# Transposes taken one by one from a list of those due, between the 512-column products, in a one-core encoder block

## The chip, the core and the metric

The kernel runs on one core of a Trainium2 chip. Time is device time in microseconds (us). The kernel before takes 1980.33 us, the median of 3 runs (1980.31 to 1980.41).

## What is computed

One encoder layer on 256 tokens of 2048 channels, float32:

```python
x = x + 0.5 * swiglu(rmsnorm(x), w_gate1, w_up1, w_down1)      # hidden layer 5632
h = rmsnorm(x)
u, v, g = split(h @ w_in)                                      # 1024, 2048, 4096 columns
a = pool_branch(u)          # centred window means by 4 groups, w_group, scale, w_proj
b = conv_branch(v)          # GLU, depthwise conv 31, LayerNorm, silu, w_proj
x = x + (sigmoid(g_a) * a + sigmoid(g_b) * b) @ w_out
x = x + 0.5 * swiglu(rmsnorm(x), w_gate2, w_up2, w_down2)
out = rmsnorm(x)
```

Nearly all of the work is matrix products of 256 tokens with the weights, 378 MB that pass through once.

## The kernel before

**Tiling.** The weights come as one stream of chunks. A chunk is two row tiles of 128 x 1024. A `Unit` is a run of chunks that adds up to x[256, K] @ w[K, 1024]: 8 chunks for K = 2048, 22 for the down projections, 4 for the two projections of the branches (K = 1024). Each row tile is split on the way into a high part wh (a cast on ScalarE, L135) and a low part wl (a subtraction on VectorE, L137), and so is each left operand. A product is one matmul of 512 columns at L208. Each row tile takes 12 of them, in `products` (L203): two token tiles t, three pairs of high and low parts, two column halves c. So a chunk has 24 products.

**Accumulators.** The two token tiles of a unit have an accumulator each (two PSUM banks), and three such buffers take turns. The second token tile of a unit is given the buffer that held the first token tile of the unit before. In the last chunk of a unit the 12 products of token tile 0 come first, then those of token tile 1.

**Order.** `run` writes for every chunk: the loads of a later chunk on SP's queue, the split of the next chunk (two casts on ScalarE, two subtractions on VectorE), then the small work that was put down for this chunk with `at`, then the chunk's products; small work put down with `amid` stands between the 12th and the 13th product. Each engine takes its instructions in the order in which they are written.

**Transposes.** The products need their left operand with channels on partitions. `transposes` (L245) takes one of two PSUM banks (pool `ps_t`), and writes four 128 x 128 transposes into it one after the other (L250): two column blocks of two token tiles. Its callers read the bank at once:

- hT: the feed-forward's hidden layer (`gate_done`, L288). Each of the 22 units of the two gate/up stages gives two groups of four, before the products of the second and of the third chunk of the next unit. One cast and one subtraction of 128 x 512 read the bank.
- xt: the residual (`x_transposed`, L254), after each half of the first feed-forward's residual and of the mixer's. Two banks in a row, so eight transposes, before the products of a chunk. Each bank is read by two pairs of a ScalarE operation (L241) and a VectorE operation (L242).
- gT: the gated convolution input (L383), eight in the middle of a chunk, read by one ScalarE copy for each bank (L385).
- mT: the gated sum of the two branches (`cp_done`, L615), eight in the middle of a chunk, read by two pairs of cast and subtraction (mAh, mAl or mBh, mBl) for each bank. The mT of the first half stand in the third and in the fourth, which is the last, chunk of the second w_cp unit. After that chunk `cp_done` adds a row to the accumulators of this unit on VectorE (L606, conv<-acc), token tile 0 first, and so gives the buffers back. The next unit is the first of w_out.

Of the kernel before, what the change touches and what calls it, by code (L numbers as in the profile page):

```python
# [13 lines left out]
P = 128  # L14
D = 2048
T = 256
NT = T // P
# [17 lines left out]
WARM = 9  # L35
# after these row tiles of weights, the row tiles of x^T that are loaded
XT_LOADS = {(0, 0): (1, 2), (0, 1): (2, 4), (1, 0): (4, 8), (2, 0): (8, 12), (3, 0): (12, 16)}
TAPS = 6
TAPS_BUSY = 4

# columns of the packed per-partition vectors
V_N1, V_NM, V_N2 = 0, KD, 2 * KD
# [8 lines left out]
class Unit:  # L51
    """x[T, K*128] @ w[K*128, 1024]: K row tiles, two banks of 512 columns for each token tile."""

# [5 lines left out]
class Special:  # L59
    """A chunk of the weight stream with a use of its own."""  # L60

# [5 lines left out]
def encoder_kernel(ctx: ExitStack, tc: tile.TileContext, x, xT, vecs, rows, pool_m,  # L67
                   w_g1, w_d1, w_in, w_pg, w_pp, w_cp, w_out, w_g2, w_d2, out):
    nc = tc.nc
# [9 lines left out]

    # ---------------------------------------------------------------- constants and small state  # L80
    ident = const.tile([P, P], F32, name="ident")
# [10 lines left out]

    # ---------------------------------------------------------------- the stream of weight chunks
    stream = []
    side, middle = {}, {}

    def at(i, fn):
        """fn is emitted before the products of chunk i."""
        side.setdefault(i, []).append(fn)

    def amid(i, fn):
        """fn is emitted between the products of chunk i."""
        while isinstance(stream[i][0], Special):
            i += 1
        middle.setdefault(i, []).append(fn)
# [60 lines left out]
    def bank(name):  # L166
        return ps_t.tile([P, C], F32, tag="T", name=name)

    def run_chunk(i):
        u, cc = stream[i]  # L170
        if isinstance(u, Special):
            u.use(split.pop(i))
            return
        if cc == 0:
            n = NT + 1 if u.tail else NT
            u.acc = [ps_a.tile([P, 2, C], F32, tag="acc", name=f"acc{i}_{t}") for t in range(n)]
        ws = split.pop(i)
        left = u.k // 2 - 1 - cc
        if u.tail and left < 2:
            # the last two chunks: token tile 0, then token tile 1 by columns  # L180
            for kk in range(2):
                products(u, 2 * cc + kk, 0, ws[kk])
            if left:
                u.kept = ws
                return
            u.tail(0, (0, 1), u.acc[0])
            for c in range(2):
                for kk in range(4):
                    products(u, 2 * cc - 2 + kk, 1, (u.kept + ws)[kk], (c,))
                u.tail(1, (c,), u.acc[1 + c])  # L190
            return
        order = [(kk, t) for kk in range(2) for t in range(NT)]
        if not left:
            order.sort(key=lambda o: o[1])
        for n, (kk, t) in enumerate(order):
            if n == 2:
                for fn in middle.pop(i, []):
                    fn()
            products(u, 2 * cc + kk, t, ws[kk])
        if not left:  # L200
            u.done(u.acc)

    def products(u, k, t, w, cs=(0, 1)):  # L203
        xh, xl = u.lhs(k, t)
        wh, wl = w
        for n, (a, b) in enumerate(((xh, wh), (xh, wl), (xl, wh))):
            for c in cs:
                nc.tensor.matmul(  # L208
                    u.acc[t + c if u.tail and t else t][:, c, :],
                    lhsT=a,  # L210
                    rhs=b[:, c * C:(c + 1) * C],
                    start=k == 0 and n == 0,
                    stop=k == u.k - 1 and n == 2,
                )

    # ---------------------------------------------------------------- operands of the products
    def pair(pool, tag, n, name):
        """hi and lo by row tile, four row tiles to a block."""
        r = []
        for b in range(n // 4):  # L220
            h, l = (block(pool, f"{tag}{s}{b}", F32R, f"{name}{s}{b}") for s in "hl")
            r += [(h[:, q, :], l[:, q, :]) for q in range(4)]
        return r
# [4 lines left out]
    def hidden(pool, name):  # L228
        """The feed-forward's hidden layer, hi and lo by row tile, four of them in a block."""
        return [tuple(block(pool, f"h{s}{u}", F32R, f"{name}{s}{u}") for s in "hl") for u in range(FF // C)]  # L230
# [7 lines left out]
    def scaled_split(dst, src, gain):  # L238
        """dst = hi and lo of src * gain, a scalar of each partition."""
        h, l = dst  # L240
# [3 lines left out]

    def transposes(src_of, n, name):  # L245
        """n (up to 4 / NT) tiles [T, 128] into one bank as [128, T] each."""
        b = bank(name)
        for j in range(n):
            for t in range(NT):
                nc.tensor.transpose(out=b[:, j * T + t * P: j * T + (t + 1) * P],  # L250
                                    in_=src_of(j, t), identity=ident)
        return b

    def x_transposed(dst, gain_base, k0):  # L254
        """dst[k0], dst[k0 + 1] = the transposed residual times the gain."""
        b = transposes(lambda j, t: X[t][:, (k0 + j) * P:(k0 + j + 1) * P], 2, f"xt{Pos.now}_{k0}")
        for j in range(2):
            scaled_split(dst[k0 + j], b[:, j * T:(j + 1) * T], vcol(gain_base, k0 + j))

# [11 lines left out]

    # ---------------------------------------------------------------- feed-forward
    def ffn_units(w_g, w_d, xt, ht, rs, residual_done, tail=None):
# [3 lines left out]
        def gate_done(u):  # L277
            def done(acc):
# [9 lines left out]
                def put(k0):  # L288
                    b = transposes(lambda j, t: hs[t][:, (k0 + j) * P:(k0 + j + 1) * P], 2,
                                   f"hT{Pos.now}_{k0}")  # L290
                    hi_lo(b.rearrange("p (q t) -> p q t", q=2), *(h[:, k0:k0 + 2, :] for h in ht[u]))
                at(Pos.now + 2, lambda: put(0))
# [19 lines left out]
    def next_operand(xt, gain_base, rs):  # L312
        """After each half of the residual: its transposed tiles, and in the end the row norms."""
        def f(half):
# [6 lines left out]

    # ---------------------------------------------------------------- pass 0: what starts the stream
    xt1 = pair(xtp, "x", KD, "xt1")
# [20 lines left out]

    # ---------------------------------------------------------------- plan
    def run(first, last):
# [9 lines left out]

    # phase 1
    ht_stack = ExitStack()
# [5 lines left out]

    # phase 2 units are appended before phase 1 runs, so that the weights run ahead
    mix = {}
# [5 lines left out]
    def v_done(j):  # L372
        def done(acc):
# [9 lines left out]
            def put(k0):  # L383
                b = transposes(lambda q, t: gl[t][:, (k0 + q) * P:(k0 + q + 1) * P], 2, f"gT{j}_{k0}")
                nc.scalar.copy(out=mix["gluT"][:, 4 * j + k0:4 * j + k0 + 2, :],  # L385
                               in_=b.rearrange("p (q t) -> p q t", q=2))
            amid(Pos.now + 1, lambda: put(0))
# [41 lines left out]
    def ln_mean():  # L429
        """LayerNorm over the channels (partitions and tiles), spread over the chunks from here."""  # L430
        cv, cp = mix["conv"], conv_pairs()
# [93 lines left out]
    def use_pool_m(ws):  # L525
        """pooled^T = u^T M^T, M the window's sum less count times the token itself."""
        def group(g):
# [69 lines left out]
    def cp_done(half):  # L597
        def done(acc):
# [16 lines left out]
            def put(k0):  # L615
                b = transposes(lambda q, t: gates[half, t][:, (k0 + q) * P:(k0 + q + 1) * P], 2,
                               f"mT{half}_{k0}")
                for q in range(2):
                    hi_lo(b[:, q * T:(q + 1) * T], *mix["m"][8 * half + k0 + q])
            for q in range(4):  # L620
# [33 lines left out]

    # phase 3 units
    ht2 = []
    fin = {}

    def final_tail(t, cs, acc):
        """The last of the residual, its norm and what is stored, for columns cs of token tile t."""  # L660
        pieces = [(c, 0, C) for c in cs] if t == 0 else [(c, a, T) for c in cs for a in (0, T)]
# [35 lines left out]

    # ---------------------------------------------------------------- run
    xr = [block(htp, f"h{s}{FF // C - 1 - j}", F32, f"xr{s}{j}") for j in range(2) for s in "hl"]
# [44 lines left out]
def _pack(w, cols):  # L744
    """[K*128, N] -> [units, K, 128, 1024]: cols[u] lists the column ranges of unit u."""
    import numpy as np
# [9 lines left out]
def _pool_constants():  # L756
    """M^T by window (tokens on partitions), and one over the counts."""
    import numpy as np
# [68 lines left out]
```

## Time and profile before

| | |
|---|---|
| median of 3 runs | 1980.33 us |
| span of the profiled execution, first to last instruction | 1978.6 us |
| what the median has beyond that span | 1.7 us |
| TensorE busy | 1966.4 us, 99% |
| VectorE busy | 1110.4 us, 56% |
| ScalarE busy | 874.5 us, 44% |
| transposes | 288: 176 hT, 64 xt, 32 mT, 16 gT |

The profile is of one execution. Of this execution the page gives the span alone, so its own time is read as the span and the 1.7 us around it. A busy TensorE says only that something was in its pipe; how long one instruction holds the engine is read from the distance between the starts of its instructions in the timeline. The timeline merges instructions of one kind that follow one another, with their count (x2, x8).

### The profile page before, as it was taken

To read this page: it belongs to the slowest core of one execution; us is meant where nothing else is said; L and a number is where in the kernel's file an instruction comes from. 1 tells how busy PE (TensorE), PEld (TensorE's weight loads), DVE (VectorE), ACT (ScalarE), POOL (GpSimd) and SP (SyncE) were. 2 spreads that over 40 slices of the span, in tenths; PEclk is the share of its full clock that TensorE was granted. 3 is DMA by queue.
4 is the path that set the end of the run, shared out by engine and by line. 5 is a ranking of instruction groups with operands and counts; after the bars stand their busy time and mean duration, and the time that the engine had idled before them with its cause. 6 is when DMAs were issued, how large, how long until landed. Compare 5 with 4: busy or idle time off the path is not lost.

```text
span 1978.6 us, 22916 instructions
## 1 busy us (share of the span) xinstructions
PE 1966.4 (99%) x8848; PEld 1629.5 (82%) x8848; DVE 1110.4 (56%) x1224; ACT 874.5 (44%) x997; POOL 11.0 (1%) x22
## 2 busy tenths in 40 slices
PE   9999999999999999999999999999999999999998
PEld 7888888888888888888888888888888888888886
DVE  5454544444445445888897765555544444444444
ACT  6444444444434345454444544544444444443433
POOL 0000000000000000000000000000000000000000
PEclk9999999999999999999999999999999999999999
DMA  8555555555555656666666555555555555565564
GB/s 310 193 188 196 190 192 188 187 189 190 192 191 187 195 189 202 194 195 211 202 208 205 184 185 185 181 186 198 191 188 189 189 190 192 181 198 195 192 192 149
DMA packets 106141, 383.88 MB, mean 194 GB/s; under 512 B 11920, under 2 KB 12176, under 8 KB 105776
## 3 DMA queue, kind: packets, MB, share of 16 engines
q1 hardware_dynamic: 104688, 378.45, 58.4%
q0 software_dynamic: 1056, 3.83, 0.6%
q8 instruction: 69, 1.13, 0.2%
q14 instruction: 40, 0.33, 0.1%
q10 hardware_dynamic: 288, 0.14, 0.0%
HBM read 380.28 MB, written 2.10 MB: 193 GB/s over the span
## 4 chain that ended last, share of the span: by engine, by line
PE 99%; DMA 1%; issue 0%; ACT 0%; DVE 0%; DVEq 0%; POOLq 0%; POOL 0%; ACTq 0%
PE acc L208 96%; PE hT L250 1%; PE xt L250 0%; DMA raw<-in_w_g 0%; PE mixb L560 0%; DMA xrh<-in_xT 0%; PE pool L535 0%; PE mT L250 0%; PE gT L250 0%; ACT fsq L668 0%; ACT wh L135 0%; PE ln_mean L442 0%; PE ln_var L471 0%; DVE X L680 0%; DVE X L665 0%
## 5 line engine op out<-in xcount | busy, mean ns | idle before, releaser
L137 DVE TENSOR_TENSOR wl<-raw,wh 128x1024 fp32r<-128x1024 f32 (+1 forms) x706 | 853.8, 1221 | 741.7 <-ACT wh L135 741.5
L135 ACT CAST wh<-raw 128x1024 fp32r<-128x1024 f32 (+1 forms) x706 | 736.2, 1050 | 906.9 <-PE acc L208 849.6
L208 PE MATMUL acc<-wh,xt1h 128*128 128x512 f32 x704 | 219.2, 392 | 1.8 <-ACT wh L135 0.9
L208 PE MATMUL acc<-wh,xt3h 128*128 128x512 f32 x704 | 218.9, 392 | 0.0
L208 PE MATMUL acc<-wl,xt1h 128*128 128x512 f32 x704 | 217.4, 390 | 0.1
L208 PE MATMUL acc<-wl,xt3h 128*128 128x512 f32 x704 | 217.1, 390 | 0.0
L208 PE MATMUL acc<-wh,xt1l 128*128 128x512 f32 x704 | 216.9, 389 | 0.0
L208 PE MATMUL acc<-wh,xt3l 128*128 128x512 f32 x704 | 216.8, 389 | 0.0
L208 PEld LDWEIGHTS acc<-wl,xt1h 128*128 128x128 f32 x704 | 132.1, 188 | 28.1 <-DVE wl L137 0.4
L208 PEld LDWEIGHTS acc<-wh,xt1l 128*128 128x128 f32 x704 | 132.1, 188 | 28.2 <-DVE xt1l L242 0.5
L208 PEld LDWEIGHTS acc<-wh,xt3l 128*128 128x128 f32 x704 | 132.1, 188 | 27.8
L208 PEld LDWEIGHTS acc<-wl,xt3h 128*128 128x128 f32 x704 | 132.1, 188 | 27.8
L208 PEld LDWEIGHTS acc<-wh,xt1h 128*128 128x128 f32 x704 | 130.6, 188 | 28.6 <-ACT wh L135 1.5
L208 PEld LDWEIGHTS acc<-wh,xt3h 128*128 128x128 f32 x704 | 130.5, 188 | 25.8
L208 PE MATMUL acc<-wh,xt2h 128*128 128x512 f32 x448 | 138.3, 390 | 0.0
L208 PE MATMUL acc<-wl,xt2h 128*128 128x512 f32 x448 | 138.1, 389 | 0.0
L208 PE MATMUL acc<-wh,xt2l 128*128 128x512 f32 x448 | 138.0, 389 | 0.0
L208 PE MATMUL acc<-wh,ht2h 128*128 128x512 f32 x352 | 109.2, 390 | 0.0
L208 PE MATMUL acc<-wl,ht2h 128*128 128x512 f32 x352 | 109.1, 389 | 0.0
L208 PE MATMUL acc<-wh,ht2l 128*128 128x512 f32 x352 | 109.0, 389 | 0.0
L208 PE MATMUL acc<-wh,ht1h 128*128 128x512 f32 x352 | 108.7, 390 | 0.0
L208 PE MATMUL acc<-wh,ht1l 128*128 128x512 f32 x352 | 108.4, 389 | 0.0
(144 smaller groups left out, 1699.9 us busy)
## 6 DMA issues: line engine op xcount, KB each, us to landing
raw<-in_w_g SPq DMA_DIRECT2D x350, 512.0 KB, 3.3
raw<-in_w_d SPq DMA_DIRECT2D x176, 512.0 KB, 3.5
raw<-in_w_in SPq DMA_DIRECT2D x112, 512.0 KB, 4.2
raw<-in_w_out SPq DMA_DIRECT2D x32, 512.0 KB, 4.2
raw<-in_w_pp SPq DMA_DIRECT2D x16, 512.0 KB, 4.0
raw<-in_w_cp SPq DMA_DIRECT2D x16, 512.0 KB, 4.0
row<-in_rows POOLq DMA_DIRECT2D x7, 512.0 KB, 4.2
X<-in_x SPq DMA_DIRECT2D x2, 1024.0 KB, 8.9
```

The lines of the kernel that those rows point to most:

```text
L135: nc.scalar.copy(out=h, in_=src)
L137: nc.vector.tensor_tensor(out=l, in0=src, in1=h.bitcast(F32), op=ALU.subtract)
L208: nc.tensor.matmul(u.acc[t + c if u.tail and t else t][:, c, :], lhsT=a, rhs=b[:, c * C:(c + 1) * C], start=k == 0 and n == 0, stop=k == u ...
L250: nc.tensor.transpose(out=b[:, j * T + t * P: j * T + (t + 1) * P], in_=src_of(j, t), identity=ident)
```

## The change

`transposes` no longer issues anything. It puts its transposes into a list `between`, and whoever reads the bank is now a function that is called behind the last transpose of the bank. `products` takes one transpose off the list after each 512-column product:

```diff
+    between = []
...
     def products(u, k, t, w, cs=(0, 1)):
...
             for c in cs:
                 nc.tensor.matmul(
...
                 )
+                if between:
+                    between.pop(0)()
...
-    def transposes(src_of, n, name):
-        b = bank(name)
-        for j in range(n):
-            for t in range(NT):
-                nc.tensor.transpose(out=b[:, j * T + t * P: j * T + (t + 1) * P],
-                                    in_=src_of(j, t), identity=ident)
-        return b
+    def transposes(src_of, n, name, use):
+        got = []
+
+        def one(j, t):
+            if not got:
+                got.append(bank(name))
+            nc.tensor.transpose(out=got[0][:, j * T + t * P: j * T + (t + 1) * P],
+                                in_=src_of(j, t), identity=ident)
+            if (j, t) == (n - 1, NT - 1):
+                use(got[0])
+        between.extend(lambda j=j, t=t: one(j, t) for j in range(n) for t in range(NT))
```

The callers for hT, xt, gT and mT hand what they did with the bank over as `use`, for hT:

```diff
-                    b = transposes(lambda j, t: hs[t][:, (k0 + j) * P:(k0 + j + 1) * P], 2,
-                                   f"hT{Pos.now}_{k0}")
-                    hi_lo(b.rearrange("p (q t) -> p q t", q=2), *(h[:, k0:k0 + 2, :] for h in ht[u]))
+                    transposes(lambda j, t: hs[t][:, (k0 + j) * P:(k0 + j + 1) * P], 2, f"hT{Pos.now}_{k0}",
+                               lambda b: hi_lo(b.rearrange("p (q t) -> p q t", q=2),
+                                               *(h[:, k0:k0 + 2, :] for h in ht[u])))
```

On TensorE the first group of hT, ahead of chunk 9, stands like this before (hT9 is the bank, h7 the hidden layer of two token tiles, acc8 the accumulators, wh9 and wl9 the weights, xt1h and xt1l the left operand; x2 are the two column halves):

```order
L250 MATMUL hT9_0_584<-ident_78,h7_0_504 128x128
L250 MATMUL hT9_0_584<-ident_78,h7_1_508 128x128
L250 MATMUL hT9_0_584<-ident_78,h7_0_504 128x128
L250 MATMUL hT9_0_584<-ident_78,h7_1_508 128x128
L208 MATMUL acc8_0_546<-wh9_0_515,xt1h0_90 128x512 x2
L208 MATMUL acc8_0_546<-wl9_0_516,xt1h0_90 128x512 x2
L208 MATMUL acc8_0_546<-wh9_0_515,xt1l0_91 128x512 x2
```

and like this after:

```order
L209 MATMUL acc8_0_546<-wh9_0_515,xt1h0_90 128x512
L256 MATMUL hT9_0_585<-ident_78,h7_0_504 128x128
L209 MATMUL acc8_0_546<-wh9_0_515,xt1h0_90 128x512
L256 MATMUL hT9_0_585<-ident_78,h7_1_508 128x128
L209 MATMUL acc8_0_546<-wl9_0_516,xt1h0_90 128x512
L256 MATMUL hT9_0_585<-ident_78,h7_0_504 128x128
L209 MATMUL acc8_0_546<-wl9_0_516,xt1h0_90 128x512
L256 MATMUL hT9_0_585<-ident_78,h7_1_508 128x128
L209 MATMUL acc8_0_546<-wh9_0_515,xt1l0_91 128x512 x2
```

The four transposes moved behind the first, second, third and fourth product of the chunk; each now has a product on both sides.

The second place is the second mT group, in the middle of chunk 205, the last of the second w_cp unit. On TensorE before (mT0_4 and mT0_6 are the two banks, gate0 the gated sum, acc202_1 the accumulator of token tile 1, yh and yl the left operand; in brackets, the engines whose semaphores an instruction waits for):

```order
L250 MATMUL mT0_4_8558<-ident_78,gate0_0_6769 128x128 [waits DVE_49,PE_49]
L250 MATMUL mT0_4_8558<-ident_78,gate0_1_6772 128x128
L250 MATMUL mT0_4_8558<-ident_78,gate0_0_6769 128x128
L250 MATMUL mT0_4_8558<-ident_78,gate0_1_6772 128x128
L250 MATMUL mT0_6_8567<-ident_78,gate0_0_6769 128x128 [waits DVE_49,PE_49]
L250 MATMUL mT0_6_8567<-ident_78,gate0_1_6772 128x128
L250 MATMUL mT0_6_8567<-ident_78,gate0_0_6769 128x128
L250 MATMUL mT0_6_8567<-ident_78,gate0_1_6772 128x128
L208 MATMUL acc202_1_8417<-wh205_0_8484,yh1_7163 128x512 x2
```

and after, from the fifth product of token tile 1 on:

```order
L209 MATMUL acc202_1_8417<-wh205_0_8484,yl1_7164 128x512
L256 MATMUL mT0_6_8572<-ident_78,gate0_0_6769 128x128 [waits DVE_49,PE_49]
L209 MATMUL acc202_1_8417<-wh205_0_8484,yl1_7164 128x512
L256 MATMUL mT0_6_8572<-ident_78,gate0_1_6772 128x128
L209 MATMUL acc202_1_8417<-wh205_1_8488,yh1_7163 128x512
L256 MATMUL mT0_6_8572<-ident_78,gate0_0_6769 128x128
L209 MATMUL acc202_1_8417<-wh205_1_8488,yh1_7163 128x512
L256 MATMUL mT0_6_8572<-ident_78,gate0_1_6772 128x128
L209 MATMUL acc202_1_8417<-wl205_1_8489,yh1_7163 128x512 x2
```

The last transpose of the second bank moved from ahead of all twelve products to behind the eighth. The order of the instructions on ScalarE, VectorE, GpSimd and SP is the same before and after, at all places; only TensorE's changes. The first product of the w_out unit into its second token tile (six products into the unit) waits for VectorE, before and after.

## Rows read from the trace of the kernel before

**Rows 1.** The page's first line, its busy times by engine, and the shares of the chain that ended last.

```profile
span 1978.6 us, 22916 instructions
...
PE 1966.4 (99%) x8848; PEld 1629.5 (82%) x8848; DVE 1110.4 (56%) x1224; ACT 874.5 (44%) x997; POOL 11.0 (1%) x22
...
PE 99%; DMA 1%; issue 0%; ACT 0%; DVE 0%; DVEq 0%; POOLq 0%; POOL 0%; ACTq 0%
```

**Rows 2.** The view of waits for TensorE, complete: who waited for whom, us in total, times, longest.

```profile
PE warm L707 <- DVE ones L326: 1.1, 1, 1.1
PE acc L208 <- ACT wh L135: 0.9, 1, 0.9
PE acc L208 <- ACT xt1h L241: 0.9, 1, 0.9
```

**Rows 3.** The transposes by the tile that they write: count, shortest, median and longest ns from start to end of one, first and last start in us.

```profile
L250 PE MATMUL hT<-ident,h x176: 270/272/273, 57.4 to 1740.6; 128*128 128x128 f32 x176
...
L250 PE MATMUL xt<-ident,X x64: 270/272/273, 622.8 to 1251.3; 128*128 128x128 f32 x64
...
L250 PE MATMUL gT<-ident,glu x16: 270/273/273, 787.0 to 832.1; 128*128 128x128 f32 x16
...
L250 PE MATMUL mT<-ident,gate x32: 270/272/273, 1138.1 to 1168.8; 128*128 128x128 f32 x32
```

**Rows 4.** The timeline of TensorE's matmuls around a group of four hT: start, us from the first start to the last end, operation, count. Two products stand in a row, so the distance between two rows' starts is two products.

```profile
56.51 0.62 PE L208 MATMUL acc<-wl,xt1h 128*128 128x512 f32 x2
56.97 0.62 PE L208 MATMUL acc<-wh,xt1l 128*128 128x512 f32 x2
57.43 0.60 PE L250 MATMUL hT<-ident,h 128*128 128x128 f32 x4
57.78 0.71 PE L208 MATMUL acc<-wh,xt1h 128*128 128x512 f32 x2
58.33 0.63 PE L208 MATMUL acc<-wl,xt1h 128*128 128x512 f32 x2
58.80 0.62 PE L208 MATMUL acc<-wh,xt1l 128*128 128x512 f32 x2
```

**Rows 5.** The same around a group of eight xt.

```profile
622.33 0.62 PE L208 MATMUL acc<-wh,ht1l 128*128 128x512 f32 x2
622.79 1.03 PE L250 MATMUL xt<-ident,X 128*128 128x128 f32 x8
...
624.12 0.63 PE L208 MATMUL acc<-wl,ht1h 128*128 128x512 f32 x2
```

**Rows 6.** The timeline of ScalarE and VectorE behind the group of four hT of rows 4; in brackets the engine's idle time ahead of the instruction and what ended it.

```profile
58.58 0.58 ACT L135 CAST ht1h<-hT 128x512 fp32r<-128x512 f32 x1
...
59.85 0.68 DVE L137 TENSOR_TENSOR ht1l<-hT,ht1h 128x512 fp32r<-128x512 f32 x1
...
60.83 1.05 ACT L135 CAST wh<-raw 128x1024 fp32r<-128x1024 f32 x1 [1.67 <-PE acc L208]
```

**Rows 7.** The timeline of ScalarE and VectorE around the group of eight xt of rows 5.

```profile
620.65 4.65 DVE L137 TENSOR_TENSOR wl<-raw,wh 128x1024 fp32r<-128x1024 f32 x4 [1.81 <-ACT wh L135]
...
625.22 0.48 DVE L242 SCALAR_TENSOR_TENSOR xt2l<-xt,vec,xt2h 128x256 fp32r<-128x256 f32 x1
...
625.73 0.84 ACT L241 ACTIVATE xt2h<-xt,vec 128x256 fp32r<-128x256 f32 x2 [1.32 <-DVE xt2l L242]
```

**Rows 8.** The timeline of TensorE, ScalarE and VectorE from the second mT group, in the last chunk of the second w_cp unit (ends at 1148.06), into the first w_out unit.

```profile
1144.45 1.03 PE L250 MATMUL mT<-ident,gate 128*128 128x128 f32 x8
...
1145.09 0.37 ACT L135 CAST mAh<-mT 128x256 fp32r<-128x256 f32 x1 [2.01 <-PE mT L250]
...
1145.49 0.43 DVE L137 TENSOR_TENSOR mAl<-mT,mAh 128x256 fp32r<-128x256 f32 x1 [0.97 <-ACT mAh L135]
...
1145.79 0.62 PE L208 MATMUL acc<-wl,yh 128*128 128x512 f32 x2
1145.95 0.65 ACT L135 CAST mAh<-mT 128x256 fp32r<-128x256 f32 x2 [0.49 <-DVE mAl L137]
...
1147.14 0.37 ACT L135 CAST mAh<-mT 128x256 fp32r<-128x256 f32 x1 [0.54 <-DVE mAl L137]
...
1147.55 0.42 DVE L137 TENSOR_TENSOR mAl<-mT,mAh 128x256 fp32r<-128x256 f32 x1 [0.44 <-ACT mAh L135]
...
1147.89 2.34 DVE L606 TENSOR_TENSOR conv<-acc,row 128x1024 f32<-128x1024 f32 x2
1148.06 0.62 PE L208 MATMUL acc<-wh,mAh 128*128 128x512 f32 x2
...
1149.42 0.62 PE L208 MATMUL acc<-wh,mAh 128*128 128x512 f32 x2
...
1150.15 2.35 DVE L137 TENSOR_TENSOR wl<-raw,wh 128x1024 fp32r<-128x1024 f32 x2
```

**Rows 9.** The timeline of TensorE and ScalarE at the first gT group.

```profile
786.95 1.03 PE L250 MATMUL gT<-ident,glu 128*128 128x128 f32 x8
...
787.59 1.07 ACT L385 COPY gluT<-gT 128x512 f32<-128x512 f32 x2 [0.58 <-PE gT L250]
...
788.55 1.06 ACT L135 CAST wh<-raw 128x1024 fp32r<-128x1024 f32 x1
```

More of the change, by code (lines that the diff above doesn't have):

```diff
@@ L243, in scaled_split, with use @@
                                        op0=ALU.mult, op1=ALU.subtract)
-    def transposes(src_of, n, name):
-        b = bank(name)
-        for j in range(n):
-            for t in range(NT):
-                nc.tensor.transpose(out=b[:, j * T + t * P: j * T + (t + 1) * P],
-                                    in_=src_of(j, t), identity=ident)
-        return b
+    def transposes(src_of, n, name, use):
[8 more added lines that the diff above has]
+        between.extend(lambda j=j, t=t: one(j, t) for j in range(n) for t in range(NT))
     def x_transposed(dst, gain_base, k0):
-        b = transposes(lambda j, t: X[t][:, (k0 + j) * P:(k0 + j + 1) * P], 2, f"xt{Pos.now}_{k0}")
-        for j in range(2):
-            scaled_split(dst[k0 + j], b[:, j * T:(j + 1) * T], vcol(gain_base, k0 + j))
+        def use(b):
+            for j in range(2):
+                scaled_split(dst[k0 + j], b[:, j * T:(j + 1) * T], vcol(gain_base, k0 + j))
+        transposes(lambda j, t: X[t][:, (k0 + j) * P:(k0 + j + 1) * P], 2, f"xt{Pos.now}_{k0}", use)
     def squares(t, slot, c0, c1):
@@ L383, in put @@
             def put(k0):
-                b = transposes(lambda q, t: gl[t][:, (k0 + q) * P:(k0 + q + 1) * P], 2, f"gT{j}_{k0}")
-                nc.scalar.copy(out=mix["gluT"][:, 4 * j + k0:4 * j + k0 + 2, :],
-                               in_=b.rearrange("p (q t) -> p q t", q=2))
+                transposes(lambda q, t: gl[t][:, (k0 + q) * P:(k0 + q + 1) * P], 2, f"gT{j}_{k0}",
+                           lambda b: nc.scalar.copy(out=mix["gluT"][:, 4 * j + k0:4 * j + k0 + 2, :],
+                                                    in_=b.rearrange("p (q t) -> p q t", q=2)))
             amid(Pos.now + 1, lambda: put(0))
@@ L615, in put, with use @@
             def put(k0):
[L616 to L619, printed above, removed]
+                def use(b):
+                    for q in range(2):
+                        hi_lo(b[:, q * T:(q + 1) * T], *mix["m"][8 * half + k0 + q])
+                transposes(lambda q, t: gates[half, t][:, (k0 + q) * P:(k0 + q + 1) * P], 2,
+                           f"mT{half}_{k0}", use)
             for q in range(4):
```

## The prediction

> **What bounds the kernel now.** First the page's busy times and the chain that ended last: TensorE is busy for 1966.4 of 1978.6 us and makes up 99% of the chain [rows 1]. Then the waits of TensorE: three, 2.9 us in all, each with a count of one, and in them no transpose [rows 2]. So TensorE is never kept waiting by a bank or by its readers, and there is no such wait for this change to remove. What it can change is how long 288 transposes hold TensorE, and whether the later readers of the banks make it wait where it doesn't now. A busy share can't tell the first, since a transpose is recorded with 272 ns [rows 3] while eight of them take 1.03 us [rows 5]. So the distances between starts are read.
>
> **What a transpose costs in a group.** The undisturbed rhythm: from 1145.79 to 1148.06 ten products start, 0.227 us each [rows 8]. Around a group of four, the product pair ahead starts at 56.97 and the second pair behind at 58.33 [rows 4]: 1.36 us, less four products (0.908), leaves 0.452 us. Around a group of eight, 622.33 to 624.12 [rows 5]: 1.79 - 0.908 = 0.882 us. With 176 hT in 44 groups of four and 64 xt, 16 gT and 32 mT in 14 groups of eight [rows 3], taking hT and xt for their sizes, the transposes hold TensorE for 44 x 0.452 + 14 x 0.882 = 32.2 us, 0.112 us each.
>
> **What a lone transpose costs.** The trace of before has none between two products, but it shows both of its borders. Leaving: the last of four starts at 57.43 + 0.60 - 0.272 = 57.758, and the second pair behind it at 58.33 [rows 4], 0.572 us, of which two products are 0.454; so the last transpose takes 0.118 us. The last of eight: 622.79 + 1.03 - 0.272 = 623.548 to 624.12 [rows 5], again 0.118. Inside a group they follow at (1.03 - 0.272) / 7 = 0.108 [rows 5]. Arriving: from the last pair to the first transpose is 0.46 us, 0.006 more than two products [rows 4, 5]. So it is the border with products that costs, some 0.010 us on leaving and 0.006 on arriving, and the change turns one pair of borders per group into four or eight. I take 0.118 for every transpose and 0.006 once for a group, since the product between two transposes is already unsettled by the one it follows and I expect no second charge for the arrival. A group of four becomes 4 x 0.118 + 0.006 = 0.478 (+0.026), one of eight 0.950 (+0.068): 44 x 0.026 + 14 x 0.068 = 1.1 + 1.0 = **+2.1 us**. The lower bound is the price in a group, 0.112: +0. A gain is excluded as long as the leaving border is what the end of a group shows; that it isn't is a rival. The upper bound charges leaving, arriving and the slower pair behind (58.33 to 58.80 is 0.016 over two products [rows 4]) to each: 0.118 + 0.006 + 0.008 = 0.132, 38.0 us, +5.8.
>
> The Trainium skill has a rule that speaks for the change: by "TensorE: Matmul & The Clock Gate", Part 2, a weight load is pulled ahead under the matmul before it, and a load of 128 columns takes 128 / 1.2 = 107 ns. By that, the 0.108 us within a group could be loads that a 128-column transpose is too short to hide, and a product ahead of each would hide them. By the same figure, the load of the product behind a lone transpose has that transpose alone to hide under, and the gain is lost again there; the 0.118 us agrees with this second reading.
>
> **What moves on the readers' side.** With the lone price, the fourth transpose starts 4 x 0.227 + 3 x 0.118 = 1.26 us behind the point at which the group began, and the eighth 2.64 us, instead of 0.32 and 0.76. The order on ScalarE, VectorE, GpSimd and SP stays, so no DMA moves, but these engines keep their order and wait longer at the bank's readers.
>
> - hT, 44 groups: the cast at 58.58 moves to about 59.0 and ends by 59.6. Behind it on ScalarE is the cast at 60.83, which idles 1.67 us for TensorE anyway; the subtraction on VectorE starts at 59.85 as now [rows 6]. Nothing.
> - xt, 8 groups: VectorE is busy with four splits until 625.30, and so its first subtraction is at 625.22 whatever happens. The eighth transpose starts at 622.79 + 2.64 = 625.43, and casts of the second bank come behind 625.73 as now [rows 7]. Nothing.
> - gT, 2 groups: the second copy moves from about 788.1 to 790. Queued behind it on ScalarE is the cast at 788.55 [rows 9], part of the split for the next chunk but one, which VectorE then follows; TensorE asks for it some 5 us later (a chunk is 24 x 0.227 = 5.4 us). Without that lead it would cost 2 us. Nothing.
> - mT: three of the four groups stand inside a unit and have the same lead. The fourth is in the last chunk of the second w_cp unit, and behind its last subtraction VectorE has conv<-acc, which frees the accumulator that the next unit wants for its token tile 1. Now: cast 1145.09, subtraction 1145.49, next cast 1145.95; last cast 1147.14, last subtraction 1147.55, conv<-acc 1147.89, its first half over at 1147.89 + 1.17 = 1149.06; TensorE uses that buffer at 1149.42 [rows 8], 0.36 us to spare. After: the eighth transpose starts at 1144.45 + 2.64 = 1147.09; a bank's first cast comes 0.32 behind its last transpose (1144.77 to 1145.09), so at 1147.41; from that cast on 0.40 + 0.46 + 0.41 + 0.34 = 1.61 us to conv<-acc [rows 8], 1149.02; its first half is over at 1150.19, while TensorE, 0.07 later than now, wants the buffer at 1149.49. It waits 0.7 us; with the hand-over I take **+0.75 us** (0.4 if the two banks' readers overlap as they do now, 1.0 if the hand-over is slow). Behind conv<-acc stand the splits at 1150.15 [rows 8]; they end about a microsecond later than now, and the chunk that needs them begins over 5 us behind 1148.06. No second wait.
>
> **The sum.** +2.1 + 0.75 = +2.85. On this execution: span 1978.6 to 1981.45, with the 1.7 us around it (1980.33 - 1978.6) **1983.2 us**, +0.14%. A measurement of this kernel can tell about 0.2%, 4.0 us, from no change, so this counts as no change.
>
> **Rivals.**
>
> 1. *Borders add up: slower.* Each transpose pays for leaving, arriving and part of the slower product behind it, since no product gets back to its rhythm between two of them. For it: the pairs behind a group are still slow at 58.33 to 58.80 [rows 4]. Against it: the arrival is small, and part of it is counted already. Price: 0.124 to 0.132, at 0.128: 36.9 - 32.2 = +4.7, and +0.75: 1985.8. It decides from (32.2 + 4.0 - 0.75) / 288 = 0.123 us each.
> 2. *The loads are hidden: faster.* The 0.108 us within a group is mostly waiting for the next transpose's weights, and behind a 512-column product these would be there in time, so that a lone transpose takes what its 128 columns take at the products' rhythm, 0.227 / 4 = 0.057 us. That gives 288 x (0.112 - 0.057) = -15.8, and +0.75: 1965.3. This is the skill's first reading. Against it: the last transpose of a group has no other behind it and still takes 0.118 [rows 4, 5].
> 3. *No new wait at the first w_out unit.* The readers of the second mT bank are quicker than their chain, or the buffer is ready by another path: 1982.4. For it: 0.36 us is to spare now. Against it: the chain's steps are read one by one.
>
> **Chances.** The forecast 0.62, rival 1 0.20, rival 2 0.04, rival 3 0.14. Faster by over 0.2% is rival 2, 0.04; within 0.2% the forecast and rival 3, 0.76; slower rival 1, 0.20. The range runs from the price in a group with the wait (+0 + 0.75, 1981.1) to rival 1 (1985.8): 1981.0 to 1985.9. It leaves out rival 2 and the ends beyond.
>
> **What would show it.** In the timeline of the changed kernel, TensorE alternates one product and one transpose: the distance from product to next product over a transpose should be 0.345 us (0.227 + 0.118); 0.35 and more is rival 1, 0.29 rival 2. The waits of TensorE should have one new row, for VectorE's conv<-acc at L615 (or an idle gap of some 0.7 us ahead of the first w_out unit's seventh product), and none for hT, xt or gT; without it rival 3. The casts of hT should stand 0.4 us later against their chunk, and ScalarE's idle time for TensorE shrink by as much. The prediction is wrong if a lone transpose is not what the end of a group shows, or if TensorE waits in more than that one place.

## The result

The changed kernel takes 1984.04 us (median of 15 runs, 1983.84 to 1985.37), the kernel before 1980.43 us in the same series (1980.22 to 1981.10): ratio 1.0019, 95% interval 1.0011 to 1.0026. The profiled execution has a span of 1982.3 us against 1978.6 [rows 1]. So it is slower by 3.6 us where 2.85 was forecast (1983.2 us), inside the range, and just inside the 4.0 us that were counted as no change.

The busy times and the complete view of waits for TensorE after the change:

```profile
span 1982.3 us, 22916 instructions
...
PE 1969.6 (99%) x8848; PEld 1625.1 (82%) x8848; DVE 1110.5 (56%) x1224; ACT 880.1 (44%) x997; POOL 10.9 (1%) x22
```

```profile
PE acc L209 <- ACT wh L136: 1.6, 1, 1.6
PE warm L717 <- DVE ones L335: 1.1, 1, 1.1
PE acc L209 <- DVE conv L615: 0.7, 1, 0.7
```

The third row is new against [rows 2], and it is the one wait that was forecast. The first is at the start of the kernel and costs nothing that lasts (below).

Around the first hT group, TensorE's timeline is now:

```profile
57.05 0.62 PE L209 MATMUL acc<-wh,xt1l 128*128 128x512 f32 x2
57.50 0.40 PE L209 MATMUL acc<-wh,xt1h 128*128 128x512 f32 x1
57.73 0.28 PE L256 MATMUL hT<-ident,h 128*128 128x128 f32 x1
57.77 0.48 PE L209 MATMUL acc<-wh,xt1h 128*128 128x512 f32 x1
58.08 0.27 PE L256 MATMUL hT<-ident,h 128*128 128x128 f32 x1
58.11 0.48 PE L209 MATMUL acc<-wl,xt1h 128*128 128x512 f32 x1
58.43 0.27 PE L256 MATMUL hT<-ident,h 128*128 128x128 f32 x1
58.46 0.48 PE L209 MATMUL acc<-wl,xt1h 128*128 128x512 f32 x1
58.77 0.27 PE L256 MATMUL hT<-ident,h 128*128 128x128 f32 x1
58.80 0.70 PE L209 MATMUL acc<-wh,xt1l 128*128 128x512 f32 x2
```

A product behind a transpose is recorded as starting 0.03 us after it and with 0.48 us instead of 0.40, so its start doesn't tell when the transpose is done with; the distance used here is from transpose to transpose: 57.73 to 58.77 is three steps of 0.347 us, a product of 0.227 and 0.120 for the transpose. Averaged over all groups it is 0.119 for hT, 0.118 for gT and mT, and 0.120 for xt. In the group a transpose took 0.108 and the last one 0.118 [rows 4, 5].

The readers' side, ScalarE behind the same group:

```profile
59.08 0.59 ACT L136 CAST ht1h<-hT 128x512 fp32r<-128x512 f32 x1 [0.34 <-PE hT L256]
60.93 1.05 ACT L136 CAST wh<-raw 128x1024 fp32r<-128x1024 f32 x1 [1.26 <-PE acc L209]
```

The cast now waits 0.34 us for the transposes, and the idle time behind it shrinks from 1.67 [rows 6] to 1.26: absorbed. At the border of the second w_cp and the first w_out unit it is not:

```profile
1148.45 0.27 PE L256 MATMUL mT<-ident,gate 128*128 128x128 f32 x1
...
1149.49 0.62 PE L209 MATMUL acc<-wh,mAh 128*128 128x512 f32 x2
...
1150.02 0.42 DVE L138 TENSOR_TENSOR mAl<-mT,mAh 128x256 fp32r<-128x256 f32 x1 [0.44 <-ACT mAh L136]
1150.37 2.34 DVE L615 TENSOR_TENSOR conv<-acc,row 128x1024 f32<-128x1024 f32 x2
...
1151.73 0.70 PE L209 MATMUL acc<-wh,mAh 128*128 128x512 f32 x2 [0.70 <-DVE conv L615]
```

From the last transpose to conv<-acc it is 1.92 us; the chain of the prediction has 0.32 + 1.61. The unit starts at 1149.49, its seventh product would come 6 x 0.227 = 1.36 us later at 1150.85, and comes at 1151.73. That is 1.36 us behind the start of conv<-acc, where the prediction has 1.17 for the first half and 0.05 for the hand-over.

How much later the same product starts in the changed kernel than in the kernel before, worked out from the starts of all 8448 products in both traces, and what each stretch adds:

| stretch | added, us | forecast |
|---|---|---|
| the kernel's start | 0.08 | 0 |
| 44 hT groups of four | 1.47 (0.033 each) | 1.1 |
| 8 xt groups of eight | 0.67 (0.083 each) | 0.54 |
| 2 gT groups of eight | 0.15 (0.077 each) | 0.14 |
| 4 mT groups of eight | 0.30 (0.074 each) | 0.27 |
| the wait at the first w_out unit | 0.96 | 0.75 |
| last product | 3.6 | 2.85 |

### The profile page after: what moved, and what is told of

Same layout as the page of the kernel before. It is cut to its first block, busy times and chain, and to the rows that moved or that the text cites. A ratio compares the mean times of both kernels' runs of the same rounds, so it can differ in the third digit from the quotient of the medians.

```text
span 1982.3 us, 22916 instructions
## 1 busy us (share of the span) xinstructions
PE 1969.6 (99%) x8848; PEld 1625.1 (82%) x8848; DVE 1110.5 (56%) x1224; ACT 880.1 (44%) x997; POOL 10.9 (1%) x22
## 4 chain that ended last, share of the span: by engine, by line
PE 99%; issue 0%; DMA 0%; DVE 0%; ACT 0%; DVEq 0%; POOLq 0%; POOL 0%; ACTq 0%
PE acc L209 97%; PE hT L256 1%; PE xt L256 0%; PE mixb L569 0%; DMA xrh<-in_xT 0%; PE pool L544 0%; PE mT L256 0%; PE gT L256 0%; ACT fsq L678 0%; DVE conv L615 0%; PE ln_mean L451 0%; PE ln_var L480 0%; ACT mAh L136 0%; DVE X L690 0%; DVE X L675 0%
## 5 line engine op out<-in xcount | busy, mean ns | idle before, releaser
L209 PE MATMUL acc<-wl,xt1h 128*128 128x512 f32 x704 | 222.1, 396 | 0.0
L209 PE MATMUL acc<-wl,xt3h 128*128 128x512 f32 x704 | 221.7, 395 | 0.0
L209 PE MATMUL acc<-wl,ht1h 128*128 128x512 f32 x352 | 109.4, 392 | 0.0
```

The costliest lines, as they stand in the source:

```text
L209: nc.tensor.matmul(u.acc[t + c if u.tail and t else t][:, c, :], lhsT=a, rhs=b[:, c * C:(c + 1) * C], start=k == 0 and n == 0, stop=k == u ...
```

## The experiments

**The wait undone.** In the changed kernel the one mT group in the last chunk of the second w_cp unit is issued at once, as a group. (`now` makes `transposes` run its list instead of storing it; it serves the other runs too.)

```diff
-    def transposes(src_of, n, name, use):
+    def transposes(src_of, n, name, use, now=False):
...
-                           f"mT{half}_{k0}", use)
+                           f"mT{half}_{k0}", use, now=half == 0 and k0 >= 4)
```

> The changed kernel, but the one mT group in the last chunk of the second w_cp unit stands as a group of eight again. Theory (its last transpose came late, and the accumulator's reader on VectorE behind it): TensorE's wait for conv<-acc disappears, 0.88 us, and seven borders of the group with it, 0.08 us: 1984.04 - 0.96 = 1983.1. Rival (the wait has another cause, such as the cast or VectorE being behind from earlier): the wait stays and the time is 1983.9 to 1984.0.

1983.1 us, 0.9 less than the changed kernel, ratio to the kernel before 1.0014 (1.0005 to 1.0023); the wait is gone from the view. VectorE and TensorE:

```profile
1149.33 2.35 DVE L620 TENSOR_TENSOR conv<-acc,row 128x1024 f32<-128x1024 f32 x2
```

```profile
1149.52 0.62 PE L209 MATMUL acc<-wh,mAh 128*128 128x512 f32 x2
...
1150.88 0.62 PE L209 MATMUL acc<-wh,mAh 128*128 128x512 f32 x2
```

The buffer's reader starts ahead of the unit again, and the seventh product comes 1.36 us into it, unhindered. Theory held, to 0.1 us.

**The wait alone.** The kernel before, with only that group taken one by one.

```diff
-    def transposes(src_of, n, name, use, now=False):
+    def transposes(src_of, n, name, use, now=True):
...
-                           f"mT{half}_{k0}", use, now=half == 0 and k0 >= 4)
+                           f"mT{half}_{k0}", use, now=half or k0 < 4)
```

> The kernel before, with the one mT group in the last chunk of the second w_cp unit taken one by one and all other groups as before. Theory (late readers hold the accumulator): TensorE waits for conv<-acc as in the changed kernel, 0.87 us, and the group's borders add 0.08: +0.95, 1981.4. Rival (the wait needs the delays that the other groups bring along): within 0.2 of the kernel before.

1981.40 us against 1980.55, ratio 1.0005 (0.9996 to 1.0014), which by itself is not clear of no change. The trace is:

```profile
1150.13 0.70 PE L209 MATMUL acc<-wh,mAh 128*128 128x512 f32 x2 [0.70 <-DVE conv L620]
```

The same wait of 0.70 us stands in the same place without any of the other spread groups, and by the products' starts this stretch adds 1.05 us. Both directions agree: eight transposes in one chunk cost about 1 us of the 3.6.

**Two at a time.** All mT in groups again; hT, xt and gT two behind a product.

```diff
-                if between:
+                for _ in range(min(2, len(between))):
                     between.pop(0)()
```

> The changed kernel with all mT in groups again and hT, xt, gT taken two at a time behind a product. Theory (each change between product and transpose costs 0.011 us, so what counts is how many there are): one border more than before for a group of four, three for a group of eight: 44 x 0.011 + 10 x 0.036 = +0.85, so 1981.3. Rival (a transpose costs more wherever it stands among products, however many stand together): as with single ones, +2.3: 1982.7.

1980.65 against 1980.47, ratio 1.0000 (0.9991 to 1.0009): neither, it is nearly free. By the products' starts it adds 0.17 us in all: 0.12 at the kernel's start, -0.10 for hT, 0.05 for xt and 0.09 for the two gT groups, whose 0.05 each stand against 0.077 with single ones. TensorE in the trace:

```profile
63.46 0.39 PE L209 MATMUL acc<-wh,xt1h 128*128 128x512 f32 x1
63.69 0.38 PE L256 MATMUL hT<-ident,h 128*128 128x128 f32 x2
63.82 0.48 PE L209 MATMUL acc<-wh,xt1h 128*128 128x512 f32 x1
64.14 0.38 PE L256 MATMUL hT<-ident,h 128*128 128x128 f32 x2
64.27 0.71 PE L209 MATMUL acc<-wl,xt1h 128*128 128x512 f32 x2
64.82 0.62 PE L209 MATMUL acc<-wh,xt1l 128*128 128x512 f32 x2
```

From pair to pair 0.45 us, less a product 0.223 us for two, 0.112 each: the price in a group of four before. So "0.011 us for each border" is not the rule. A stop of the products has a price of its own, and it depends on how the rhythm comes back.

**All behind the first product.**

```diff
-                if between:
+                while between:
                     between.pop(0)()
```

(All mT in groups as well.)

> The changed kernel with all mT in groups again and the whole list taken behind the first product. Theory (borders): as many borders as before, each group moved by one product, so 1980.4 within 0.3. Rival (it is the place, between products of one chunk instead of between chunks, that costs): up to the +2.3 of single ones, 1982.7.

1980.52 against 1980.47, ratio 1.0000 (0.9991 to 1.0009). By the products' starts nothing is added behind the kernel's start, which by itself differs by -0.2 to +0.8 us from trace to trace. Moving the transposes costs nothing; spreading them does.

**Every second product.** All mT in groups again.

```diff
+    between_at = [0]
...
-                if between:
+                between_at[0] += 1
+                if between and between_at[0] % 2 == 0:
                     between.pop(0)()
```

> The changed kernel with all mT in groups again and one transpose behind every second product only. Theory (a border costs the same whatever the distance): hT, xt and gT as in the changed kernel, +2.3, so 1982.7. Rival (the second product behind a transpose is slow as well, 0.006 us as behind a group, and each single transpose pays for it when it has two products to itself): 256 x 0.006 = 1.5 more, 1984.2.

1983.68, ratio 1.0016 (1.0007 to 1.0025), nearer to the rival. In the trace:

```profile
63.77 0.28 PE L258 MATMUL hT<-ident,h 128*128 128x128 f32 x1
63.80 0.71 PE L210 MATMUL acc<-wl,xt1h 128*128 128x512 f32 x2
64.35 0.27 PE L258 MATMUL hT<-ident,h 128*128 128x128 f32 x1
64.38 0.71 PE L210 MATMUL acc<-wh,xt1l 128*128 128x512 f32 x2
64.92 0.27 PE L258 MATMUL hT<-ident,h 128*128 128x128 f32 x1
64.95 0.71 PE L210 MATMUL acc<-wh,xt1h 128*128 128x512 f32 x2
65.50 0.27 PE L258 MATMUL hT<-ident,h 128*128 128x128 f32 x1
```

63.77 to 65.50 is three steps of 0.577 us; less two products, 0.123 us for each transpose, more than with one product between. This fits the rival, a second slow product behind each transpose, and with it the mechanism of the prediction's rival 1; which of the two products is the slow one, these rows don't show. By the products' starts hT adds 0.054 us a group (0.033 in the changed kernel) and gT 0.106 (0.077), but xt 0.078 (0.083), so it is not dearer everywhere.

**What a lone matmul pays for.** 120 extra matmuls, two for each bank of hT and xt, each alone between two products (gT and mT in groups); NARROW is 16, then 128, with one ahead of each of the first two transposes:

```diff
+        def narrow(a, b):
+            if not got:
+                got.append(bank(name))
+            nc.tensor.matmul(got[0][:, :NARROW], lhsT=a, rhs=b, start=True, stop=True)
...
                 if between:
-                    between.pop(0)()
+                    between.pop(0)(a, b[:, :NARROW])
```

With 16 and 128 columns the second extra matmul of a bank overwrites columns of the first transposed tile, so the operands made from that tile are not the reference's. With 256 columns both stand ahead of the first transpose and all is computed.

> Measures what a short matmul between two products costs by its width. As the changed kernel with gT and mT in groups, plus 120 extra matmuls of 16 columns, each with the weights and the columns of the product ahead of it, put into the bank that the transposes then write over; each stands alone between two products. Theory A (a lone matmul takes at least the weight load of the product behind it, whatever its width): product to product over one is 0.227 + 0.11 = 0.34 us. Theory B (it takes its columns): 0.227 + 0.01 to 0.03, so 0.24 to 0.26 us.

> The same with 128 columns. Theory A: 0.34 us again, as with 16 columns and as with a transpose. Theory B: 0.227 + 0.057 to 0.07, so 0.28 to 0.30 us, and a transpose's 0.119 is then its own stream.

> As with 16 and 128 columns, now 256 columns, with both extra matmuls of a bank ahead of its first transpose. The 16 columns took 0.113 us and the 128 columns 0.117 us between two products. Theory A (what is paid is the weight load of the product behind, and columns that pass in the same time are free): 256 columns at the products' rhythm are 0.227 / 2 = 0.114 us, so 0.115 to 0.125 us, product to product 0.34 to 0.35. Theory B (a fixed price and the columns on top): 0.113 + 0.107 = 0.22 us, 0.45.

From an extra matmul to the transpose that stands one product behind it, 16 columns (with PEld, the weight load of that product), then 128 columns:

```profile
58.96 0.17 PE L257 MATMUL hT<-wl,xt1h 128*128 128x16 f32 x1
58.96 0.19 PEld L210 LDWEIGHTS acc<-wl,xt1h 128*128 128x128 f32 x1
58.98 0.47 PE L210 MATMUL acc<-wl,xt1h 128*128 128x512 f32 x1
...
59.30 0.27 PE L262 MATMUL hT<-ident,h 128*128 128x128 f32 x1
```

```profile
58.23 0.22 PE L257 MATMUL hT<-wl,xt1h 128*128 128x128 f32 x1
58.29 0.45 PE L210 MATMUL acc<-wl,xt1h 128*128 128x512 f32 x1
58.57 0.27 PE L262 MATMUL hT<-ident,h 128*128 128x128 f32 x1
```

and 256 columns, from one extra matmul to the next:

```profile
57.88 0.28 PE L257 MATMUL hT<-wh,xt1h 128*128 128x256 f32 x1
57.99 0.40 PE L210 MATMUL acc<-wh,xt1h 128*128 128x512 f32 x1
58.22 0.28 PE L257 MATMUL hT<-wh,xt1h 128*128 128x256 f32 x1
```

0.34 us each time, and over all 120 of a run, less a product, in the mean 0.120, 0.118 and 0.123 us. The whole times agree: 1996.28, 1995.44 and 1997.33 us, single runs, within 2 us of one another for 120 extra matmuls whose columns differ sixteenfold; had 240 more columns been paid for at the products' rhythm, 240 / 512 x 0.227 x 120 = 12.8 us would lie between the first and the last. Theory A held, theory B fell: up to 256 columns, what stands alone between two products costs about 0.12 us, nearly whatever its width. That this is the load of the next product's weights is the reading that fits: the load is the same in all three, and it is recorded as starting with the short matmul ahead of its product and not before (58.96 in the first rows). But the load itself was not timed apart, and a least time of some 0.11 us for any matmul would give the same distances; no run tells the two apart.

**The other way: fewer stops.** The kernel before with the two groups of four hT merged into one of eight, at the start of the chunk; then the same in mid-chunk with xt moved there too; then the fours moved without merging.

```diff
                 at(Pos.now + 2, lambda: put(0))
-                at(Pos.now + 3, lambda: put(2))
+                at(Pos.now + 2, lambda: put(2))
```

```diff
-                at(Pos.now + 2, lambda: put(0))
-                at(Pos.now + 3, lambda: put(2))
+                amid(Pos.now + 2, lambda: put(0))
+                amid(Pos.now + 2, lambda: put(2))
...
-                at(n + 2 + q // 2, lambda q=q: x_transposed(xt, gain_base, 8 * half + 2 * q))
+                amid(n + 2 + q // 2, lambda q=q: x_transposed(xt, gain_base, 8 * half + 2 * q))
```

```diff
-                at(Pos.now + 2, lambda: put(0))
-                at(Pos.now + 3, lambda: put(2))
+                amid(Pos.now + 2, lambda: put(0))
+                amid(Pos.now + 3, lambda: put(2))
```

> The kernel before, with the two groups of four hT of a unit merged into one of eight, at the start of the chunk where the first stood. Theory (what is saved is one stop of the products and what follows it, 0.040 to 0.060 us, wherever the group stands): 22 x 0.06 = -1.3, 1979.2, as with the group in mid-chunk. Rival (the place in mid-chunk gave part of it, since behind a group at the chunk's start the products are slow for longer): a long stretch of slow products stays behind each eight and it is 22 x 0.033 = -0.7, 1979.8.

> The kernel before, the other way round: the two groups of four hT of a unit become one of eight, and all hT and xt groups stand between the 12th and the 13th product of their chunk. Theory (borders): 22 borders fewer, 0.011 us each, -0.24, and behind a group in mid-chunk the slow products are fewer in the trace (gT and mT: 0.893 us for eight with what follows, xt at a chunk's start 0.921, two hT groups 0.954), so 22 x 0.061 + 8 x 0.028 = -1.6 in all: 1978.9. Rival (what follows a group doesn't depend on its place): -0.24 to -0.5, 1980.0 to 1980.2.

> The kernel before with the groups of four hT moved as they are to between the 12th and the 13th product. Theory (what follows a group is shorter in mid-chunk): 44 groups with 0.010 instead of 0.028 us of slow products behind: -0.8, 1979.6. Rival (the place doesn't matter): 1980.4.

The expectation for eights at the start was written when the results of the two in mid-chunk were known.

| | us | kernel before beside it | ratio |
|---|---|---|---|
| eights at the start | 1979.20 | 1980.55 | 0.9993 (0.9984 to 1.0002) |
| eights and xt in mid-chunk | 1979.28 | 1980.66 | 0.9994 (0.9985 to 1.0003) |
| fours in mid-chunk | 1980.46 | 1980.66 | 0.9999 (0.9990 to 1.0008) |

The place does nothing, so the reason given for mid-chunk falls: fours in mid-chunk came out as their rival, and eights and xt in mid-chunk fell between theory and rival. Merging saves: by the products' starts 0.060 us for each unit at either place, 1.3 us in all, as the theory for eights at the start has it, though no interval alone excludes no change. Behind a four (fours in mid-chunk) and behind an eight (eights at the start) TensorE goes on like this:

```profile
60.08 0.60 PE L250 MATMUL hT<-ident,h 128*128 128x128 f32 x4
60.44 0.71 PE L208 MATMUL acc<-wh,xt1h 128*128 128x512 f32 x2
60.98 0.63 PE L208 MATMUL acc<-wl,xt1h 128*128 128x512 f32 x2
61.45 0.62 PE L208 MATMUL acc<-wh,xt1l 128*128 128x512 f32 x2
61.91 0.62 PE L208 MATMUL acc<-wh,xt1h 128*128 128x512 f32 x2
62.37 0.62 PE L208 MATMUL acc<-wl,xt1h 128*128 128x512 f32 x2
```

```profile
58.23 1.03 PE L250 MATMUL hT<-ident,h 128*128 128x128 f32 x8
59.02 0.71 PE L208 MATMUL acc<-wh,xt1h 128*128 128x512 f32 x2
59.57 0.62 PE L208 MATMUL acc<-wl,xt1h 128*128 128x512 f32 x2
60.02 0.62 PE L208 MATMUL acc<-wh,xt1l 128*128 128x512 f32 x2
```

Behind this four, three pairs from 60.98 to 62.37 take 0.463 us each; behind this eight the pair at 59.57 is back at 0.45. It is not the number alone: the products behind an eight of xt stay slow at either place, by 0.04 us beyond the first pair, those behind an eight of hT by 0.004.

## Why the prediction held, step by step

- **No wait to remove.** Right: TensorE waited for no transpose before, and nothing was gained.
- **The price of a lone transpose** was read from the border at a group's end: 0.118, measured 0.118 to 0.120. The price was right; the term built on it is too small by 0.5 us in all (2.1 forecast, 2.59 measured over hT, xt, gT and mT). The prediction counts up to the second pair behind a group. By the products' starts, a group of four hT takes 0.480 us after up to there, for 0.478 forecast (0.1 us over 44 groups), and one of eight xt 0.968, for 0.950 (0.15 over 8). The products behind that pair, which the sum leaves out, are slow for another 0.030 us after and 0.024 before (hT; gT and mT 0.012 and 0.004), some 0.25 over all groups. In all it is (32.2 + 2.59) / 288 = 0.121 us for a transpose, between the forecast and rival 1 (from 0.123 each), which was narrowly not reached.
- **The hidden load** (rival 2) did not come: 0.118 to 0.120 us for a lone transpose, not 0.057. The lone matmuls of 16 to 256 columns show what stands against it: they cost about 0.12 us too, and so a transpose gains nothing from a product ahead of it.
- **The readers' side.** Right at all four kinds: nothing for hT, xt and gT; one wait of 0.70 us at the first w_out unit for 0.7 forecast, so rival 3 fell. The term of 0.75 measured 0.96. At the seventh product itself the delay grows by 0.86: it starts 1.36 us behind the start of conv<-acc, for 1.17 + 0.05 in the chain (half of two merged rows and the hand-over). The other 0.09 are the products behind the wait, slow until their rhythm is back, which the sum did not have. Both terms of the sum came out too small, so the total was not right by errors that cancel.
- **What was not seen.** The sum over borders is too simple. Pairs cost nothing where they replace a four of hT, but over half of the single price in gT; hT and gT taken two products apart cost more than one apart; and the slow products behind a stop have no one length. Why they take the time they do stays open.

## What to carry to other kernels

Hiding a short matmul's own weights behind a wide one does not make it free: read the distance from the last short one of a group to the third product behind it, less two products, for in this kernel that is what every lone one paid, within 0.002 us. Keep short matmuls together, and merge groups where the readers and banks allow it. When work is spread out in time, look for the place where its last piece is followed in its reader's queue by something that the next stage waits for; here one of 58 groups cost about 1 us, the 57 others together 2.5.

## What the runs showed of the hardware that was not expected

- A matmul of 16, 128 or 256 columns between two 512-column products took the same 0.34 us with one of them, 0.227 without: in the mean of 120 each, 0.120, 0.118 and 0.123 us (16, 128 and 256 columns).
- After the stops of transposes and after the wait, the products need a stretch of differing length to get back to 0.227 us each: pairs at 0.46 to 0.47 us for several pairs behind a four, none behind an eight in the rows above, several behind an eight of xt. In the rows above, taking two transposes at a time between products cost 0.112 us each, one at a time 0.120, and one at every second product 0.123.
